# Input norm's factor multiplied onto the projection's results, the first two column groups taken together, and the filters' first layers in five overlapping steps

## The chip, the core and the metric

The kernel runs on one core of a Trainium2 chip, as one program on five engines: TensorE (PE) multiplies matrices, VectorE (DVE) and ScalarE (ACT) work elementwise, GpSimd (POOL) helps with a few elementwise steps, and SyncE (SP) issues most of the transfers. The metric is the device time of one execution in microseconds (us), the median of several runs. All engines run their own list of instructions in order and wait for each other through semaphores.

## The reference, cut to what matters

One encoder layer over 2048 positions of width 1024, all in float32. The part that the change touches is its beginning: a norm over the rows of the input, one wide projection, a width-3 convolution over the positions, and the network that makes the filters of the long convolutions.

```python
def _rms_norm(x, g):
    y = xf * lax.rsqrt(jnp.mean(xf * xf, axis=-1, keepdims=True) + EPS)
    return (y * g.astype(jnp.float32)).astype(x.dtype)
...
        u = _rms_norm(h, norm_mix_g[l])
        proj = u @ w_in[l]
        hy = _short_conv_centred(proj[..., :HY_COLS], hy_conv_w[l], hy_conv_b[l])
...
    hid = jnp.sin(fr1.astype(f32) * (z @ w1.astype(f32) + b1.astype(f32)))
    hid = jnp.sin(fr2.astype(f32) * (hid @ w2.astype(f32) + b2.astype(f32)))
    filt = (hid @ w3.astype(f32)).reshape(L, HYENA_ORDER, FILTER_DIRS, D_HYENA)
```

After that come the long convolutions (the hyena group) by transforms of 64 by 64 points, a gated recurrence over chunks (mLSTM), an output projection, cross-attention into 256 memory tokens and a squared-ReLU feed-forward layer. None of these is changed.

## The kernel before, in words

**Two-part products.** A float32 operand is split into a high part (`xh`, `wh`) in the matmul's own type and the rest (`xl`, `wl`). Each product is three matmuls (`mm3`, lines 340 to 342): high by high, high by low, low by high. For the split, ScalarE writes the high part and VectorE subtracts it from the source (`split`, line 345).

**The sweep.** `sweep` makes the projection transposed, with output channels on partitions and positions along the free axis. It goes by column groups `c2` of 256 channels. For each, four accumulations of 24 matmuls of 128x512 each are made: `c` is one of two chunks of 512 positions, `m` one of two halves of the 256 channels. I call one such accumulation a product group; it fills one of four `mm` banks of the matmul memory. A group's result is copied by ScalarE into a row buffer `P` (line 687). When both chunks of a channel block are there, the width-3 convolution is made from `P` into `cv` (one ScalarE and two VectorE instructions, lines 701 to 704), and later `sweep_out` transposes `cv` on TensorE and writes it out. The program makes the first half of the positions (`hf` = 0) for column groups 0 to 3, then the second half for the same ones: 16 and 16 product groups. Between the two, `x_chunk` loads and normalises the other 1024 positions into the same `xh` and `xl`.

**The beginning.** `x_first` loads 512 positions of x (`x0`), sums the squares over the 1024 channels (ScalarE squares, VectorE adds, one small matmul over the partitions, line 539), takes the inverse root on VectorE with eleven instructions of four columns (`rsqrt`), spreads the 512 factors over all partitions by a matmul with a diagonal (`spread`, line 456), multiplies x by gain and factor (`gained`, line 464), and only then splits it into `xh` and `xl`. The other 512 positions (`x1`) are treated the same; their sums come from a second copy of x in its natural layout, which ScalarE squares and sums along the rows (`square_sum`, line 421).

**The filters.** `filters` first makes the hidden layer `hid` in four column pieces, each with two matmuls (lines 267 and 271) and two sines; a sine is six VectorE instructions and one of ScalarE. Then come 32 steps: two matmuls into `pf` and `pb` (`hy<-fw,hid`), two VectorE multiplications by the decay window (lines 317 and 318), a sum on VectorE (line 322), a difference on GpSimd, and four transform matmuls (`hy<-b,f`).

**What sets the order.** `program` weaves generators by hand-set weights: the sweep with the filters, then the hyena group with the rest of the projections. A scheduler then reorders the instructions by its own simulated times within what data and buffers allow, except those pinned by `keep_in_program_order`. The hyena group begins with `spectrum` (line 879 on): 32 matmuls `hy<-a,f`, whose inputs are read from and whose results are written to device memory.

Of the kernel before, what the change touches and what calls it, by code (L numbers as in the profile page):

```python
# [10 lines left out]
F32 = mybir.dt.float32  # L11
# [122 lines left out]
class Prog:  # L134
    def __init__(self, ctx, tc, a):
# [19 lines left out]
        self.mid = None  # L155
# [78 lines left out]
    def filters(self):  # L234
# [3 lines left out]
        if True:  # L238
            fw = sb.tile([128, 1280], F32, name="fw")
            nc.scalar.dma_start(out=fw, in_=a["fw"])  # L240
# [3 lines left out]
            nc.scalar.dma_start(out=f1, in_=a["c_f1"])  # L244
# [16 lines left out]
            for c in range(4):  # L261
                yield 2
                cs = slice(512 * c, 512 * c + 512)
                feat = tb()
                nc.sync.dma_start(out=feat[0:66], in_=a["c_feat"][:, cs])
                p1 = self.hy()
                nc.tensor.matmul(p1, w1, feat[0:66], start=True, stop=True)
                hid1 = tb()
                sine(hid1, p1, 0, 1, c == 0)
                p2 = self.hy()  # L270
                nc.tensor.matmul(p2, w2, hid1, start=True, stop=True)
                sine(hid.rearrange("p j (g m) -> p m g j", g=2)[:, 16 * c:16 * c + 16], p2, 2, 3)
# [215 lines left out]
    def x_first(self):  # L488
        nc, sb = self.nc, self.isb
        pin = self.tc.keep_in_program_order  # L490
        c0, c1 = slice(0, 512), slice(512, 1024)

        def write(xs, cs, rb, between=lambda k: None):
            for k in range(9):
                if k < 8:
                    d = self.gained(xs[k], self.g_mix[:, k:k + 1], rb)
                    if k:
                        pin(d)
                    pin(nc.scalar.copy(self.xh[:, k, cs], xs[k]))
                if k:  # L500
                    nc.vector.tensor_tensor(self.xl[:, k - 1, cs], xs[k - 1], self.xh[:, k - 1, cs].bitcast(F32), ALU.subtract)
                between(k)

        def pieces(ts):
            return [ts[k // 2][:, k % 2] for k in range(8)]

        x0 = []
# [4 lines left out]
        wsrc = self.items[0][0].rearrange("(k p) c -> p k c", p=128)  # L512
        w0 = [sb.tile([128, 8, 256], F32R, tag=tag, name=tag, bufs=2) for tag in ("wh", "wl")]
        raw = [self.ta().rearrange("p k c -> p (k c)").rearrange("p (k c) -> p k c", k=4) for i in range(2)]
        for i in range(2):
            nc.sync.dma_start(out=raw[i], in_=wsrc[:, 4 * i:4 * i + 4])
        nat = []
        for i in range(4):
            rows = self.a["x"][512 + 128 * i:640 + 128 * i]
            if i < 2:  # L520
                xn = sb.tile([128, D], F32, tag="xn", name="xn", bufs=2)
                nc.sync.dma_start(out=xn, in_=rows)
                nat += [xn[:, 0:512], xn[:, 512:1024]]
            else:
                for h in range(2):
                    xn = self.tb()
                    nc.sync.dma_start(out=xn, in_=rows[:, 512 * h:512 * h + 512])
                    nat.append(xn)
        x1 = pieces([self.x_load(1, j, self.ta()) for j in range(4)])

        ssum = sb.tile([128, 512], F32, tag="rb", name="ssum", bufs=2)
        for k in range(8):
            sq = sb.tile([128, 512], F32, tag="st", name="sq", bufs=3) if k else ssum
            pin(nc.scalar.activation(sq, x0[k], AF.Square))
            if k:
                nc.vector.tensor_tensor(ssum, ssum, sq, ALU.add)
        p = self.mm()
        for t in range(4):
            nc.tensor.matmul(p[:, t:t + 1], ssum[:, 128 * t:128 * t + 128], self.ones[:, 0:1], start=True, stop=True)
        self.inv_rms(self.rx[:, 0:4], p[:, 0:4])  # L540
        dg = self.diagonal(self.rx[:, 0:4])
        ss = sb.tile([128, 2, 4], F32, tag="ss", name="ss", bufs=2)

        def nat_sum(i):
            self.square_sum(nat[i], ss[:, i % 2, i // 2:i // 2 + 1])

        for k in range(0, 8, 2):
            ks = slice(k, k + 2)
            self.split(w0[0][:, ks], w0[1][:, ks], raw[k // 4][:, k % 4:k % 4 + 2])
        for i in range(4):  # L550
            nat_sum(i)
        self.wst = iter((w0,))
        rb = self.spread(dg)
        later = []

        def between(k):
            if k < 4:
                nat_sum(4 + k)
            if k == 4:
                self.close_sums(self.rx[:, 4:8], ss)  # L560
                later.append(self.diagonal(self.rx[:, 4:8]))
        write(x0, c0, rb, between)

        def rest():
            write(x1, c1, self.spread(later[0], True))
            w1 = self.weights(sb, *self.items[1], kc=2, nbufs=4, pin=True)
            self.wst = self.stream(sb, self.items[2:], w1, kc=2, nbufs=4)
        self.mid = rest
        for _ in range(9):
            yield  # L570
        for c in (2, 3):
            yield from self.row_stats(self.rx[:, 4 * c:4 * c + 4], self.a["x"][512 * c:512 * c + 512])
        yield from self.row_stats(self.rm, self.a["mem"])

    def pop(self, n=1):
        for _ in range(n):
            if self.prepq is not None and next(self.prepq, 0) == 0:
                self.prepq = None

# [74 lines left out]
    def sweep(self, cols, hf, first, after=None):  # L654
        nc, a, sb = self.nc, self.a, self.isb
        xh, xl, cw, cb, carry = self.xh, self.xl, self.cw, self.cb, self.carry
        for c2 in cols:
            wh, wl = next(self.wst)
            Ps = []
# [6 lines left out]
            for c in range(2):  # L666
                for m in range(2):
# [5 lines left out]
                    for k in range(8):  # L673
                        self.mm3(p, wh[:, k, ms], wl[:, k, ms], xh[:, k, cs], xl[:, k, cs], k == 0, k == 7)
                        if k == 5 and self.mid is not None:
                            f, self.mid = self.mid, None
                            f()
                    if c == 0:
                        P = sb.tile([128, 1088], F32, tag="P", name="P", bufs=2)
                        Ps.append(P)  # L680
                        edge = 0 if hf == 0 else 1024 if first else 1041
                        nc.vector.memset(P[:, edge:edge + 1], 0.0)
                        if not first:
                            e0 = 1025 if hf == 0 else 0
                            nc.vector.tensor_copy(P[:, e0:e0 + 17], cc)
                    P = Ps[m]
                    nc.scalar.copy(P[:, off + 512 * c:off + 512 * c + 512], p)
                    if c == 0:
                        if self.pending:
# [1323 lines left out]
```

## Time and profile before

| | us |
|---|---|
| median of 3 runs | 3173.7 |
| lowest and highest run | 3167.94 and 3176.09 |
| profiled execution | 3171.69 |
| its span from first to last instruction | 3169.9 |

TensorE counts as busy in 3035.0 us of the span (96%), VectorE in 2048.8, ScalarE in 1499.1. In the views below, a timeline row gives start and duration, the engine, the line of the code, the operation, output and inputs by the program's tile names, and in brackets how long the engine had stood idle and for whom. A row of a table of stages gives the length of the stage, the busy time of TensorE, of its weight loads, of VectorE, ScalarE and GpSimd with their counts, TensorE's granted clock, the share of the transfer engines that was in use, and GB/s.

### The profile page before, as it was taken

What the parts mean: (1) busy time and instruction counts of PE and PEld (TensorE: products, weight loads), DVE (VectorE), ACT (ScalarE), POOL (GpSimd) and SP (SyncE); (2) the same over time, 40 slices, a digit from 0 to 9 for tenths busy, and PEclk for the clock granted to TensorE, in tenths of its full rate; (3) what the DMA queues carried; (4) which work ended last, traced back from release to release, by engine and by line L of the source; (5) the groups of instructions that cost most, each with busy time, mean ns of one, the idle gap of its engine ahead of it and who ended that gap; (6) DMA issues with size and microseconds to landing.
All of it is one profiled execution on the core that took longest, in us unless ns stands there. A gap on an engine that the chain in (4) does not pass through costs nothing.

```text
span 3169.9 us, 43590 instructions
## 1 busy us (share of the span) xinstructions
PE 3035.0 (96%) x14473; PEld 2391.2 (75%) x14473; DVE 2048.8 (65%) x3563; ACT 1499.1 (47%) x2873; POOL 1155.0 (36%) x802
## 2 busy tenths in 40 slices
PE   6999999999899986999999999999999999999998
PEld 4655666876577866888888888888888778888876
DVE  7775466344755787877765656557555685565595
ACT  5533366424555444554454455556555443333335
POOL 0122012100112234323141426776555483434483
PEclk9999999999999988999999999999999999999999
DMA  5564877685677988546384747656644474444434
GB/s 188 191 208 160 266 204 209 176 262 183 176 217 209 275 271 258 170 147 230 122 273 147 262 138 247 206 193 225 213 146 150 167 243 145 146 127 150 124 92 170
DMA packets 447530, 609.22 MB, mean 192 GB/s; under 512 B 39102, under 2 KB 249150, under 8 KB 446280
## 3 DMA queue, kind: packets, MB, share of 16 engines
q1 hardware_dynamic: 409124, 547.92, 54.3%
q10 hardware_dynamic: 38180, 58.51, 5.6%
q8 instruction: 115, 1.88, 0.2%
q14 instruction: 111, 0.91, 0.1%
HBM read 403.88 MB, written 202.41 MB: 191 GB/s over the span
## 4 chain that ended last, share of the span: by engine, by line
PE 78%; DVE 7%; DMA 7%; ACT 3%; issue 3%; POOL 2%; SPq 0%; ACTq 0%; DVEq 0%; POOLq 0%
PE mm L340 17%; PE mm L342 17%; PE mm L341 16%; PE hy L340 5%; PE hy L342 5%; PE hy L341 5%; PE hy L177 3%; PE mm L842 1%; DVE wl L345 1%; PE hy L873 1%; PE hy L915 1%; DMA xt<-in_x_t_dram 1%; PE hy L1079 1%; DVE bl L1547 1%; PE hy L1202 1%
## 5 line engine op out<-in xcount | busy, mean ns | idle before, releaser
L345 DVE TENSOR_TENSOR wl<-wn,wh 128x512 fp32r<-128x512 f32 (+1 forms) x364 | 289.8, 839 | 99.7 <-ACT wh L345 97.8
L1547 DVE TENSOR_TENSOR bl<-wr,bh 128x512 fp32r<-128x512 f32 x213 | 239.5, 1130 | 128.8 <-ACT bh L1546 127.7
L1546 ACT CAST ah<-w 128x512 fp32r<-128x512 f32 x284 | 176.6, 623 | 302.9 <-PE hy L341 155.2
L920 POOL TENSOR_TENSOR b<-b,a 128x512 f32<-128x512 f32 x64 | 87.0, 1362 | 578.5 <-ACT b L918 484.0
L340 PE MATMUL mm<-xh,wh 128*128 128x512 f32 x640 | 274.2, 429 | 7.2 <-DVE st L205 2.8
L345 ACT CAST wh<-wn 128x512 fp32r<-128x512 f32 (+1 forms) x364 | 205.2, 618 | 154.0 <-PE mm L342 52.4
L342 PE MATMUL mm<-xh,wl 128*128 128x512 f32 x640 | 257.8, 404 | 0.0
L341 PE MATMUL mm<-xl,wh 128*128 128x512 f32 x640 | 255.7, 400 | 0.0
L1546 ACT CAST bh<-wr 128x512 fp32r<-128x512 f32 x232 | 143.7, 621 | 231.2 <-PE mm L342 175.1
L1547 DVE TENSOR_TENSOR al<-w,ah 128x512 fp32r<-128x512 f32 x236 | 215.2, 912 | 54.5 <-ACT ah L1546 54.5
L342 PE MATMUL mm<-bh,al 128*128 128x512 f32 x576 | 225.3, 394 | 7.6 <-DVE al L1547 4.8
L340 PE MATMUL mm<-bh,ah 128*128 128x512 f32 x576 | 226.9, 394 | 1.8 <-DVE acc L1704 1.7
L341 PE MATMUL mm<-bl,ah 128*128 128x512 f32 x576 | 226.1, 392 | 0.0
L341 PE MATMUL mm<-act,wh 128*128 128x512 f32 x512 | 200.4, 392 | 0.2 <-DVE act L345 0.2
L342 PE MATMUL mm<-act,wl 128*128 128x512 f32 x512 | 198.9, 391 | 0.0
L340 PE MATMUL mm<-act,wh 128*128 128x512 f32 x512 | 198.4, 394 | 0.2
L340 PE MATMUL hy<-bh,ah 128*128 128x512 f32 x448 | 175.2, 391 | 0.0
L341 PE MATMUL hy<-bl,ah 128*128 128x512 f32 x448 | 174.6, 390 | 0.0
L342 PE MATMUL hy<-bh,al 128*128 128x512 f32 x448 | 174.4, 390 | 0.0
L340 PEld LDWEIGHTS mm<-xh,wh 128*128 128x128 f32 x640 | 122.4, 191 | 65.6 <-issue 19.8
L340 PE MATMUL mm<-wh,xh 128*128 128x256 f32 (+1 forms) x512 | 154.1, 302 | 6.9 <-ACT xh L345 5.1
L341 PEld LDWEIGHTS mm<-xl,wh 128*128 128x128 f32 x640 | 121.8, 190 | 48.1 <-issue 23.7
(377 smaller groups left out, 8381.0 us busy)
## 6 DMA issues: line engine op xcount, KB each, us to landing
wr<-hc SPq DMA_DIRECT2D x224, 256.0 KB
w<-in_ff_w_dram SPq DMA_DIRECT2D x172, 256.0 KB
hc<-wn SPq DMA_DIRECT2D x128, 256.0 KB
wn<-in_w_in_dram SPq DMA_DIRECT2D x100, 256.0 KB
hc<-q SPq DMA_DIRECT2D x96, 256.0 KB
fs<-a SPq DMA_DIRECT2D x32, 512.0 KB
a<-fs SPq DMA_DIRECT2D x64, 256.0 KB
a<-zs SPq DMA_DIRECT2D x64, 256.0 KB
```

The lines of the kernel that those rows point to most:

```text
L177: b = self.nc.tensor.matmul(*products[-1], start=True, stop=True)
L340: mm(ps, lh, rh, start=start, stop=False)
L341: mm(ps, lh, rl, start=False, stop=False)
L342: mm(ps, ll, rh, start=False, stop=stop)
L345: both = (self.nc.scalar.copy(hi, src), self.nc.vector.tensor_tensor(lo, src, hi.bitcast(F32), ALU.subtract))
L842: nc.tensor.matmul(pp, dm[:, m], t[:, m], start=True, stop=True)
L873: nc.tensor.matmul(pg, em[:, m], y, start=True, stop=True)
L915: nc.tensor.matmul(pp, dm[:, m], t[:, m], start=True, stop=True)
L920: nc.gpsimd.tensor_tensor(xt, xt, hi[:, m], ALU.mult)
L1079: pin(nc.tensor.matmul(pc[:, 129 * i:129 * i + 129], kk[:, 2 * p + i], ve[:, 2 * p + i], start=True, stop=True))
L1546: self.nc.scalar.copy(hi, src)
L1547: eng.tensor_tensor(lo, src, hi.bitcast(F32), ALU.subtract)
```

## The change

**The factor moves.** In `x_first` the operand is now x times the gain alone: ScalarE writes `xh` with the gain as its scale, VectorE writes `xl` in one instruction that multiplies and subtracts. The row factor is multiplied onto the results instead: VectorE multiplies each of the first 16 product groups by `rowb` while it moves them out of the matmul memory, where ScalarE copied them before. Squares and sums of both chunks are now made from the transposed x (the natural copy is no longer loaded), after the operands.

**Two column groups together.** For the first 1024 positions, column groups 0 and 1 run together: the four product groups of chunk 0 first, then the four of chunk 1. Up to three finished groups wait in their banks before they leave (`lag`). `hooks` puts the loads, squares and factors between the matmuls of these groups, by group and step. The weights of group 1 are loaded with those of group 0.

**The filters' hidden layer** runs in five steps, in each of which one piece's first layer and the piece before's second layer are made. Its weights and the transform matrix are now loaded by SyncE, behind x, and the sweep is five groups ahead before it starts, where it was two.

```diff
-            nc.scalar.dma_start(out=fw, in_=a["fw"])
+            nc.sync.dma_start(out=fw, in_=a["fw"])
...
+            for c in range(5):
+                yield 6
+                last = hid1
+                if c < 4:
+                    p1 = self.hy()
+                    nc.tensor.matmul(p1, w1, feats.pop(0)[0:66], start=True, stop=True)
+                if c:
+                    p2 = self.hy()
+                    nc.tensor.matmul(p2, w2, last, start=True, stop=True)
+                if c < 4:
+                    hid1 = tb()
+                    sine(hid1, p1, 0, 1, c == 0)
+                if c:
+                    sine(hid.rearrange("p j (g m) -> p m g j", g=2)[:, 16 * c - 16:16 * c], p2, 2, 3)
...
+            x0.append(self.x_load(0, j, t[:, 0:D].rearrange("p (k t) -> p k t", k=2)))
+            if j % 2 == 0:
+                nc.sync.dma_start(out=raw[j // 2], in_=wsrc[:, 2 * j:2 * j + 4])
...
+        def operand(xs, c, k):
+            to = (slice(None), k, slice(512 * c, 512 * c + 512))
+            g = self.g_mix[:, k:k + 1]
+            pin(nc.scalar.activation(self.xh[to], xs[k], AF.Copy, scale=g))
+            nc.vector.scalar_tensor_tensor(self.xl[to], xs[k], g, self.xh[to].bitcast(F32), ALU.mult, ALU.subtract)
...
+        def columns(c):
+            p = self.hy()
+            for t in range(4):
+                nc.tensor.matmul(p[:, t:t + 1], ssum[c][:, 128 * t:128 * t + 128], self.ones[:, 0:1], start=True, stop=True)
+            rx = self.rx[:, 4 * c:4 * c + 4]
+            self.inv_rms(rx, p[:, 0:4])
+            self.dg = self.diagonal(rx)
+
+        def rows(c):
+            p = self.hy()
+            nc.tensor.matmul(p, self.ones, self.dg, start=True, stop=True)
+            nc.scalar.copy(self.rowb[c], p)
...
+        self.hooks = {(0, 5): second, (1, 5): operands, (2, 0): lambda: scales(0), (2, 5): lambda: squares(x1, 1),
+                      (4, 0): lambda: scales(1), (6, 0): third}
...
+        for run in [cols[:2]] + [[c2] for c2 in cols[2:]] if self.made == 0 else [[c2] for c2 in cols]:
...
+            for c, c2 in [(c, c2) for c in range(2) for c2 in run]:
...
-                    nc.scalar.copy(P[:, off + 512 * c:off + 512 * c + 512], p)
...
+                        if hf == 0 and first:
+                            nc.vector.tensor_tensor(to, p, self.rowb[c], ALU.mult)
+                        else:
+                            nc.scalar.copy(to, p)
...
+                    self.lag.append(leave)
+                    while len(self.lag) > max(0, min(3, 8 - self.made)):
+                        self.lag.pop(0)()
+                    self.made += 1
...
-            next(s)
-            next(s)
-            weave(s, p.filters(), 140, 80, True)
+            f = p.filters()
+            for _ in range(5):
+                next(s)
+            next(f)
+            weave(s, f, 140, 102, True)
```

How the instructions stand now, at three places. First SyncE's queue at the start of the program, where `xt` are the four pairs of x's first chunk, `a<-in_w_in` the halves of the first weights, `xn` and `b` the natural copy of x, `a<-in_x_t` the second chunk, `wn` the next weights. Before:

```order
L475 DMA xt<-in_x_t_dram 128x2x512 x4
L516 DMA a<-in_w_in_dram 128x4x256 x2
L522 DMA xn<-in_x_dram 128x1024 x2
L527 DMA b<-in_x_dram 128x512 x4
L475 DMA a<-in_x_t_dram 128x2x512 x4
L374 DMA wn<-in_w_in_dram 128x2x256 x4
```

And now:

```order
L486 DMA xt<-in_x_t_dram 128x2x512
L519 DMA a<-in_w_in_dram 128x4x256
L486 DMA xt<-in_x_t_dram 128x2x512 x2
L519 DMA a<-in_w_in_dram 128x4x256
L486 DMA xt<-in_x_t_dram 128x2x512
L560 DMA wn<-in_w_in_dram 128x2x256 x4
L486 DMA a<-in_x_t_dram 128x2x512 x4
L240 DMA fw<-in_fw_dram 128x1280
L244 DMA f_358<-in_c_f_dram 128x128
```

The first weights moved to second place in the queue, the natural copy is gone, and the filters' weights stand behind the second chunk.

Second, VectorE's list around the first row factors. Before, the diagonal of the first chunk (`dg`) is followed by the operand products `xt<-xt,par,rb` and the residuals `xl`:

```order
L417 COPY small<-xr_y 128x4
L450 TENSOR_SCALAR dg<-ident,small 128x128 x4
L464 SCALAR_TENSOR_TENSOR xt<-xt,par,rb 128x512 x2
L501 TENSOR_TENSOR xl<-xt,xh 128x512
L464 SCALAR_TENSOR_TENSOR xt<-xt,par,rb 128x512
```

Now the diagonal comes behind all 16 residuals, and four results (`P`, `P_97`, `P_98`) are multiplied by the row factors `rowb_95` right after it, ahead of the second chunk's sum of squares (`ssum_94`) and the next weights:

```order
L428 COPY small<-xr_y 128x4
L461 TENSOR_SCALAR dg<-ident,small 128x128 x4
L706 TENSOR_TENSOR P<-mm,rowb_95 128x512 x2
L706 TENSOR_TENSOR P_97<-mm,rowb_95 128x512
L706 TENSOR_TENSOR P_98<-mm,rowb_95 128x512
L533 TENSOR_TENSOR ssum_94<-ssum_94,sq 128x512 x7
L356 TENSOR_TENSOR wl<-wn,wh 128x512 x2
```

The release of the four banks moved from ScalarE's list to VectorE's, behind the factor's chain.

Third, TensorE's list where the hyena group's first transforms (`hy<-a,f`, 32 in all) stand among the sweep's matmuls (`mm<-xh,wh` and its like) and transposes (`mm<-ident,cv`). Before, at the 912th sweep matmul:

```order
L342 MATMUL mm<-xh,wl 128x512
L721 MATMUL mm<-ident,cv 126x128 x3
L177 MATMUL hy<-a,f_2447 128x512
L188 MATMUL hy<-a,f_2447 128x512
L721 MATMUL mm<-ident,cv 126x128 x3
L177 MATMUL hy<-a,f_2447 128x512
L188 MATMUL hy<-a,f_2447 128x512
L721 MATMUL mm<-ident,cv 126x128 x2
```

Now, at the 960th, where 28 of the 32 stand in one piece (its end is shown):

```order
L177 MATMUL hy<-a,f_2481 128x512
L188 MATMUL hy<-a,f_2481 128x512
L866 MATMUL mm<-a,dm 128x512 x2
L351 MATMUL mm<-xh,wh 128x512
L352 MATMUL mm<-xl,wh 128x512
L353 MATMUL mm<-xh,wl 128x512
```

Before, the 32 began behind the 868th sweep matmul and ended behind the 950th; now they begin behind the 949th and end behind the 960th.

More of the change, by code (lines that the diff above doesn't have):

```diff
@@ L517, in x_first @@
[L517 to L528, printed above, removed]
@@ L540, in x_first @@
[L540 to L553, printed above, removed]
@@ L554, in x_first @@
[L554 to L567, printed above, removed]
```

168 lines of the change are left out of this document (89 added, 79 removed).

## Prediction

> **What bounds the kernel now.** The page comes first. TensorE is busy almost everywhere, so only the places where it is not can be gained or lost.
>
> ```profile
> span 3169.9 us, 43590 instructions
> PE 3035.0 (96%) x14473; PEld 2391.2 (75%) x14473; DVE 2048.8 (65%) x3563; ACT 1499.1 (47%) x2873; POOL 1155.0 (36%) x802
> ```
>
> Next the table of stages over the part that the change touches, with one later stage and two stretches chosen for VectorE.
>
> ```profile
> 0.00:20.00 20.00, 2.01 (x9) 1.92 (x9) 11.32 (x35) 10.76 (x21) 0.70 (x6) 1.00 0.92 336
> 20.00:40.00 20.00, 13.95 (x25) 7.03 (x26) 15.97 (x41) 9.45 (x19) 0.00 (x0) 0.85 0.54 191
> 60.00:80.00 20.00, 18.69 (x86) 14.49 (x86) 15.89 (x28) 14.60 (x31) 0.00 (x0) 1.00 0.66 185
> 80.00:100.00 20.00, 19.01 (x85) 14.98 (x84) 16.63 (x40) 14.50 (x32) 0.00 (x0) 1.00 0.79 265
> 140.00:160.00 20.00, 15.75 (x78) 8.54 (x76) 20.00 (x47) 12.45 (x18) 3.11 (x2) 1.00 0.57 190
> 160.00:180.00 20.00, 18.71 (x67) 9.47 (x68) 19.15 (x33) 6.09 (x10) 4.82 (x3) 0.83 0.59 202
> 200.00:220.00 20.00, 20.00 (x104) 11.72 (x106) 13.29 (x20) 8.22 (x16) 5.71 (x4) 1.00 0.56 185
> 347.00:390.00 43.00, 41.00 (x169) 22.96 (x169) 19.11 (x30) 15.86 (x28) 0.00 (x0) 1.00 1.01 334
> 0.00:164.65 164.65, 132.77 (x554) 93.21 (x555) 125.44 (x265) 86.63 (x162) 11.97 (x12) 0.97 0.58 192
> 143.30:164.65 21.35, 15.81 (x68) 8.41 (x67) 21.35 (x40) 10.56 (x16) 4.28 (x2) 0.89 0.58 192
> ```
>
> TensorE does almost nothing in the first 20 us. Around 140 to 180, where x's second half is prepared, VectorE is full (20.00 and 19.15 of 20) and TensorE is not. After 200 TensorE is full again. The waits (for whom: total, times, longest) name the same two places:
>
> ```profile
> PE hy L271 <- ACT b L258: 3.9, 1, 3.9
> PE mm L456 <- DVE dg L450: 3.9, 1, 3.9
> PE hy L177 <- DVE b L318: 3.6, 1, 3.6
> ```
>
> The timeline gives the beginning:
>
> ```profile
> 5.48 0.63 ACT L534 ACTIVATE ssum<-xt 128x512 f32<-128x512 f32 x1 [1.95 <-DMA xt<-in_x_t_dram]
> ...
> 8.71 1.15 ACT L534 ACTIVATE sq<-xt 128x512 f32<-128x512 f32 x2 [2.08 <-DMA xt<-in_x_t_dram]
> ...
> 10.03 1.15 ACT L534 ACTIVATE sq<-xt 128x512 f32<-128x512 f32 x2 [0.17 <-DMA xt<-in_x_t_dram]
> ...
> 14.10 1.87 PE L539 MATMUL mm<-ones,ssum 128*128 128x1 f32 x8 [14.10 <-DVE ssum L536]
> ...
> 16.00 0.16 DVE L416 TENSOR_SCALAR ms<-mm 128x4 f32<-128x4 f32 x1 [0.15 <-PE mm L539]
> ...
> 18.93 0.87 DVE L450 TENSOR_SCALAR dg<-ident,small 128x128 f32<-128x128 f32 x4
> 19.86 2.08 PE L456 MATMUL mm<-dg,ones 128*128 128x512 f32 x2 [3.89 <-DVE dg L450]
> 21.97 0.59 ACT L460 COPY rb<-mm 128x512 f32<-128x512 f32 x1 [3.84 <-PE mm L456]
> ...
> 24.05 0.80 PE L340 MATMUL mm<-xh,wh 128*128 128x512 f32 x1 [2.11 <-ACT xh L499]
> ...
> 27.50 0.63 PE L341 MATMUL mm<-xl,wh 128*128 128x512 f32 x1
> ...
> 42.40 0.39 PE L340 MATMUL mm<-xh,wh 128*128 128x512 f32 x1
> 42.63 0.39 PE L341 MATMUL mm<-xl,wh 128*128 128x512 f32 x1
> ```
>
> The first sweep product starts at 24.05, behind squares, sums, root, diagonal and spreading. The ninth starts at 27.50, so the first ones are 0.43 apart; at 42.40 they are 0.23 apart.
>
> **The change, part by part.** I first follow the new beginning to the first multiplication of the second chunk's results, then VectorE's work from there to the reload of x, then TensorE.
>
> *Beginning.* The first pair of x lands by 5.5 and further transfers of the same size 1.3 apart (8.71 to 10.03), so the first weights, now second in the queue, land near 6.8 and TensorE starts near 7. Root and spreading no longer stand before it. The filters' weights, moved behind x, are needed only by the filters, which start behind 190 products; that cover costs nothing. The first two groups (48 products) need 12 at 0.43 and 36 at 0.23, 13.4 us, so they end at 20.4; the sixth transfer lands at 12, so they do not wait for it. In TensorE's new list the column sums stand behind product 76 (26.8). I take 1 us for them, half of 1.87, since that row ran at the slow spacing. The root and diagonal take 3.8 (16.00 to 18.93 and 0.87), to 31.5. The spread stands behind product 94, at 31.9, and takes 1 (half of 2.08); ScalarE's copy 0.6. The first row factor is there at 33.5, and the fifth group waits about 1 us for the first bank, to 34.2. Products 97 to 142, the second column sums, products 143 to 186 and the second spread follow: 10.4 + 1 + 10 + 0.9, to 56.6; with the copy, the multiplication of the fifth group starts at **57.5**. VectorE has long finished the second diagonal by then and waits: its list stands behind that spread.
>
> *VectorE's work.* Its prices, by group (busy in total, mean ns of one):
>
> ```profile
> L464 DVE SCALAR_TENSOR_TENSOR xt<-xt,par,rb 128x512 f32<-128x512 f32 x24 | 17.4, 764 | 4.1 <-ACT rb L460 2.8 <-DMA xt<-in_x_t_dram 1.3
> L345 DVE TENSOR_TENSOR wl<-wn,wh 128x512 fp32r<-128x512 f32 x20 | 12.9, 689 | 1.0 <-ACT wh L345 1.0
> L703 DVE SCALAR_TENSOR_TENSOR cv<-P,par,cv 128x1008 f32<-128x1008 f32 x8 | 10.1, 1266 | 4.8 <-ACT cv L701 4.8
> ...
> L322 DVE TENSOR_TENSOR b<-b 128x512 f32<-128x512 f32 x11 | 8.6, 786 | 0.4
> L317 DVE TENSOR_TENSOR b<-hy,a 128x512 f32<-128x512 f32 x11 | 7.6, 688 | 9.0 <-PE hy L188 9.0
> ...
> L501 DVE TENSOR_TENSOR xl<-xt,xh 128x512 fp32r<-128x512 f32 x8 | 5.4, 688 | 0.7 <-ACT xh L499 0.7
> L536 DVE TENSOR_TENSOR ssum<-ssum,sq 128x512 f32<-128x512 f32 x7 | 4.8, 692 | 7.0 <-ACT sq L534 6.5
> ```
>
> The fused residual and the multiplication of a result are not in this trace. The first is bounded by 0.69 (a plain residual) and 0.76 (the two-step `xt` product); I take 0.76, the same form. The second is bounded by 0.69 (`b<-hy,a`, a product with one input in the matmul memory) on both sides within a few hundredths, for shape and types are the same. Up to the fourth wide split of the reload, which ends at 164.65, VectorE had 125.44 us of work. Its new list has, up to the same split: 16 gain products less (12.2), 16 plain residuals less (11.0), three filter steps less, which moved behind (6 at 0.69 and 3 at 0.79, 6.5); 16 fused residuals (12.2), 16 results (11.0), 7 sums (4.8), 8 diagonals (1.7) and one `cv` (1.3) more. That is 31.0 - 29.7, so 126.7 us. Ahead of 57.5 stand 16 fused residuals, 12 `wl`, 14 sums, 8 diagonals, 4 results and 26 small ones of 0.16: 12.2 + 8.3 + 9.7 + 1.7 + 2.8 + 4.2 = 38.9. So 87.8 us are left, and the split ends at 57.5 + 87.8 = **145.3** if VectorE never waits. It was full from 143.30 to 164.65; I take 2 us of waits, between none and 20 (its share in 60 to 100 was 81%; a rival below). ScalarE is no limit: it loses 16 copies and eight row sums and was at 14.6 of 20 at most.
>
> *TensorE.* The second half's first 18 products follow that split; here is where it stood:
>
> ```profile
> 171.48 0.79 PE L340 MATMUL mm<-xh,wh 128*128 128x512 f32 x1
> ```
> ```profile
> L340 PE MATMUL mm<-xh,wh 128*128 128x512 f32 x136 | 57.5, 426 | 4.0 <-ACT xh L499 2.1 <-ACT xh L345 1.9
> ```
> ```profile
> L188 PE MATMUL hy<-fw,hid 64*128 64x512 f32 x64 | 36.6, 655 | 0.0
> ...
> L188 PE MATMUL hy<-b,f 64*64 64x512 f32 x192 | 36.1, 616 | 0.0
> ```
>
> 136 of each of the three products lie before 171.48, so this is the 409th. Now six products follow the split: 145.3 + 2 + 1.4 = 148.7, which is 22.8 earlier. But by then TensorE had done 16 `hy<-fw,hid` and 24 `hy<-b,f`, and has now done 6 and 6. All 64 of the first kind take 36.6 us (two engine rows each) and all 128 of the second 36.1, so 10 x 0.57 + 18 x 0.28 = 10.8 us are still owed. The lead is 12.0 us, and since TensorE is full from 200 on, it stays until the hyena group begins.
>
> *The hyena group's first stage.* Before, 32 `hy<-a,f` lay among 82 sweep products, and the transfer engines were at 1.01 for 43 us at 334 GB/s:
>
> ```profile
> 347.61 0.69 PE L177 MATMUL hy<-a,f 64*128 64x512 f32 x1
> ```
> ```profile
> L188 PE MATMUL hy<-a,f 64*128 64x512 f32 x32 | 16.9, 628 | 0.0
> ```
>
> Now they lie among 11 products, so about 16 us of cover are gone. The stage reads 8 x 0.5 MB and writes 16 x 0.5 MB; four reads can come ahead and three pairs of writes may end behind it, which leaves 7 MB, 21 us at 334 GB/s, against 16.9 + 2.5 us of matmuls. So the loss is between none and 16 (the stage keeps its 43 us); I take 1.4, close to the 21.
>
> Sum: 22.8 - 10.8 - 1.4 = 10.6 us against the profiled execution of 3171.7 (2 us under the median of 3173.7): **3161.1 us**. 0.3% is 9.5 us here, about what a measurement of this kernel can tell from no change.
>
> **A rule against it.** The granted clock was 0.85 in 20 to 40 and the first products were 0.43 apart for over 3.4 us. If the operands of the first two groups come with gaps and the clock stays down for all 48 products, they take 20.6 instead of 13.4, and all that follows, VectorE's wait for the second spread too, comes 7.2 later: gain 3.4, 3168. The first products before had such gaps and stayed slow for six microseconds. Against it: the new operands come every 0.7 us for two groups at once, more than slow products can use. The Trainium skill ("TensorE: Matmul & The Clock Gate", Part 1) says that the clock is halved until a whole busy window of about 3.4 us, running free of the kernel, has passed. By that page the slow stretch here would be an estimated 3.4 to 6.8 us, 8 to 16 products, which moves the sum by 1 us to either side.
>
> **Rivals.**
>
> *The lead is eaten on the way.* VectorE waits more than I take, or the hyena's first stage loses half of its cover. For: TensorE now waits for banks that VectorE's list frees in order, and 28 transforms stand in one piece. Against: full VectorE at 143 to 164, and reads that can run ahead. With 8 us of the 16 lost in that stage, 3161.1 + 6.6 = 3168; with VectorE at 92%, 6 us more, 3167.
>
> *Slower: VectorE and TensorE wait for each other in turn.* Twelve groups, the fifth to the sixteenth, now leave their banks only through VectorE's list, where sines and convolutions stand ahead of them; TensorE stops for a bank, and VectorE then stops for what TensorE has not yet made. Place: 57 to 165. If VectorE is busy only 78% of that, its 87.8 us take 112.6, 24.8 of waits instead of 2: 3161.1 + 22.8 = **3184**. It decides from 22 us of waits on, a share below 80%. For: 15.89 and 16.63 of 20 in 60 to 100, under an order made by the same rules. Against: there TensorE was the fuller one (18.69, 19.01), so VectorE could not be; when it was behind, it was full.
>
> *The clock stays down*: 3168, as above.
>
> **How the numbers follow.** The forecast has 0.47, the eaten lead 0.28, the slow clock 0.08, the mutual waits 0.17. So faster by over 0.3% 0.47, within 0.3% 0.36, slower 0.17. The forecast's own range is 3156 to 3164: no waits and no loss gives 3157.7, with 2 us for the early walk; 3 us more of waits the upper end. The range over all cases is **3154 to 3180**: below lies only an early walk that is wrong by more than 3 us (0.06), above most of the mutual waits (0.12).
>
> **What would show it.** TensorE's first sweep product near 7 us; the first multiplication onto a result near 33.5 and the fifth near 57.5; VectorE at 95% or more from there to the fourth wide split, near 147; the 409th product near 149, with 6 and 6 filter products before it; the 28 transforms in 18 to 23 us. The forecast is wrong if VectorE has idle times over 10 us in all between 57 and 147, if the transforms take 30 us or more, or if TensorE's total idle time from 400 us on, in the stages that are worded the same, grows by more than 5 us.

## The result, and the profile after

The changed kernel takes 3149.7 us (median of 6 runs, 3146.7 to 3152.8), the kernel before 3172.5 (also 6 runs): ratio 0.993, interval 0.9918 to 0.9943. So it is faster by 22.7 us, where the forecast had 10.6 (3161.1 against the profiled execution's 3171.7), and lies below the range. The two profiled executions, on which all that follows rests, took 3171.7 and 3152.8 us. First the page, whose span was 3169.9 before:

```profile
span 3151.0 us, 43589 instructions
PE 3025.6 (96%) x14481; PEld 2387.9 (76%) x14481; DVE 2054.8 (65%) x3569; ACT 1490.3 (47%) x2848; POOL 1149.4 (36%) x802
```

TensorE's work is the same, so the question is where it loses time. I count its work by giving every matmul the median distance to the next one of its kind and shape in the two kernels (2904 us in all); what a stretch takes beyond that is lost, to waits and to a slow clock alike. From here on "lost" means this. Each figure comes from one execution. Up to 340 us, kernels with the same TensorE list differ by at most 1.7 us in it. Behind the last place where lists differ (1307 to 1359 us) all fourteen kernels of this study have the same one and need 1829 to 1833 us for it. But 17 runs of the kernel before lie between 3160.0 and 3177.7 us, so a few us in one stage between 340 and 1360 prove little.

| us lost in | 0 to 200 | 200 to 340 | 340 to 420 | 420 to 700 | 700 to 1000 | 1000 to 1300 | 1300 to 3100 |
|---|---|---|---|---|---|---|---|
| before | 59.7 | 31.9 | 8.8 | 10.6 | 37.8 | 76.2 | 24.0 |
| after | 49.6 | 32.6 | 24.2 | 9.0 | 14.6 | 74.1 | 26.0 |
| difference | -10.1 | +0.7 | **+15.4** | -1.6 | **-23.2** | -2.1 | +2.0 |

The 10.1 us of the beginning, for which the forecast had 12.0, are used up by 420. The gain is made between 700 and 1000, in instructions that the change leaves as they were. The differences add up to -18.9 us, as the two spans do. The table of stages shows the same, first before, then after (behind the stage and its length comes TensorE's busy time; the last three numbers are its granted clock, the share of the transfer engines and GB/s):

```profile
340.00:420.00 80.00, 76.18 (x316) 49.37 (x315) 40.03 (x61) 35.87 (x59) 3.81 (x3) 1.00 0.89 273
700.00:1000.00 300.00, 279.70 (x1300) 200.63 (x1301) 172.44 (x365) 149.09 (x255) 41.35 (x33) 0.97 0.67 194
```
```profile
340.00:420.00 80.00, 64.58 (x271) 40.88 (x271) 33.67 (x52) 28.36 (x49) 4.29 (x3) 0.96 0.87 281
700.00:1000.00 300.00, 294.30 (x1396) 211.10 (x1396) 187.59 (x394) 161.16 (x274) 47.20 (x36) 0.99 0.76 219
```

*The beginning.* TensorE's timeline after, and VectorE's first multiplications of results:

```profile
8.97 0.80 PE L351 MATMUL mm<-xh,wh 128*128 128x512 f32 x1 [8.97 <-ACT wh L356]
...
13.83 0.63 PE L353 MATMUL mm<-xh,wl 128*128 128x512 f32 x1
14.25 0.67 PE L351 MATMUL mm<-xh,wh 128*128 128x512 f32 x2
14.76 0.39 PE L352 MATMUL mm<-xl,wh 128*128 128x512 f32 x1
...
84.52 2.07 PE L276 MATMUL hy<-b,fw 128*128 128x512 f32 x2 [6.35 <-ACT b L258]
```
```profile
36.00 2.49 DVE L706 TENSOR_TENSOR P<-mm,rowb 128x512 f32<-128x512 f32 x4 [2.39 <-ACT rowb L546]
60.37 1.89 DVE L706 TENSOR_TENSOR P<-mm,rowb 128x512 f32<-128x512 f32 x3 [6.58 <-ACT rowb L546]
```

The first product starts at 8.97, not near 7, since ScalarE loads a table (1.28 us) and makes a high part of x and of the weights first. The multiplications come at 36.0 and 60.4 (forecast 33.5 and 57.5). The slow stretch lasts from 8.97 to 14.25, 5.3 us with matmuls 0.43 apart, and none follows among the first 48 products: the rival of 48 slow products is out. The Trainium skill ("TensorE: Matmul & The Clock Gate", Part 1) has a busy window of about 3.4 us as the condition, in a window that runs free of the kernel; the 5.3 us lie within the 3.4 to 6.8 us estimated from it.

The lead is already largest at 60 us, 18 us, and falls to 8 by 100:

```profile
60.00:80.00 20.00, 17.36 (x76) 12.56 (x74) 19.63 (x38) 15.06 (x31) 0.00 (x0) 1.00 0.54 169
80.00:100.00 20.00, 13.89 (x45) 9.24 (x46) 16.58 (x55) 10.81 (x27) 0.00 (x0) 0.74 0.87 256
```
```profile
60.37:153.26 92.89, 80.29 (x333) 55.62 (x332) 85.33 (x188) 47.86 (x86) 4.21 (x2) 0.91 0.58 179
```

VectorE is full up to 80 (19.63 of 20), TensorE waits 6.35 us for a sine (row 84.52) and 1.6 for a step of a root (`ms`), and its granted clock falls to 0.74. This is close to the rival of mutual waits, but over 40 us, not 100, and for the filters' sines: for a bank that a multiplication of results frees, TensorE waits 0.4 us in all from 60 to 153. To the fourth wide split, which ends at 153.3 instead of 147.3, VectorE does 85.3 us of work in 92.9 (92%), where I had 87.8 and 2 us of waits. The 409th product starts at 145.4 (forecast 149, with the 6 and 6 filter products that were named), 7.9 us before that split ends; so it does not hang on the split, as the forecast's working has it, and TensorE's list takes other products first.

*The transforms.* They last from 360.8 to 392.5. Over that time, and TensorE's waits from 340 to 420:

```profile
360.80:392.50 31.70, 19.73 (x74) 8.20 (x75) 15.59 (x24) 11.66 (x21) 0.00 (x0) 0.95 1.04 349
```
```profile
PE hy L177 <- DMA a<-hy: 6.1, 3, 3.8
PE hy L177 <- ACT a L909: 5.8, 4, 1.9
```

With the transfer engines at 1.04 and 349 GB/s, TensorE has work for 19.7 of 31.7 us. In that time 11.1 MB were moved (31.7 times 349), not the 7 MB of the forecast.

What opens this stage is not TensorE. Its first reads (`a<-hy`) stand in SyncE's queue behind a wait for the landing of the filters' last result (`fs<-a`); as the code has it, the hyena group's pool of buffers is opened where the filters' one was closed. The reads before, then SyncE's wait and the reads after:

```profile
340.66 2.54 SPq L818 DMA_DIRECT2D a<-hy  x4
```
```profile
SPq L835 <- DMA fs<-a: 3.4, 1, 3.4
353.97 2.44 SPq L842 DMA_DIRECT2D a<-hy  x4
```

The filters start three groups later in the changed kernel, and this landing comes at 352.9 instead of 339.6. In all fourteen kernels the first read is issued 0.9 to 1.1 us behind it. Meanwhile TensorE goes on with sweep products: 838 had started when the first read was issued before, 920 now. That work is then missing beside the transforms as cover, that is, as work for TensorE while the transfers run.

*From 700 to 1000.* The longest waits before, and all above 0.3 us after:

```profile
PE mm L340 <- ACT xh L345: 5.1, 3, 3.2
PE mm L721 <- DVE a L846: 3.3, 1, 3.3
PE mm L340 <- DVE st L205: 2.8, 2, 2.3
PE mm L842 <- DMA a<-fs: 2.4, 1, 2.4
PE mm L842 <- DVE a L846: 1.9, 1, 1.9
```
```profile
PE mm L351 <- ACT xh L356: 3.5, 2, 2.7
PE mm L351 <- ACT st L203: 1.8, 1, 1.8
PE hy L897 <- DMA va<-vd: 1.5, 1, 1.5
```

The first row, waits for an operand, mostly stays. What goes are the waits for `mm` banks that VectorE empties (`a`, results of the hyena group's filter responses; `st`, transposed pieces). Such a wait can cost more than itself, as before at 798 and at 843:

```profile
797.72 0.69 PE L721 MATMUL mm<-ident,cv 128*128 128x128 f32 x4 [3.31 <-DVE a L846]
799.79 0.37 PE L727 MATMUL mm<-ident,cv 128*16 128x128 f32 x1 [1.38 <-DVE a L846]
...
803.89 0.63 PE L341 MATMUL mm<-xl,wh 128*128 128x512 f32 x1
804.32 0.63 PE L342 MATMUL mm<-xh,wl 128*128 128x512 f32 x1
...
843.27 0.80 PE L340 MATMUL mm<-xh,wh 128*128 128x512 f32 x1 [2.35 <-DVE st L205]
843.87 0.63 PE L341 MATMUL mm<-xl,wh 128*128 128x512 f32 x1
844.29 0.63 PE L342 MATMUL mm<-xh,wl 128*128 128x512 f32 x1
```

Matmuls are 0.43 apart behind the first wait until 805, and behind the one at 843 until 846; the granted clock was 0.50 from 800 to 805 and from 843 to 846. The stretch from 780 to 820 loses 9.2 us for 5.6 us of waits. The Trainium skill ("TensorE: Matmul & The Clock Gate", "Why this matters for your kernels") warns of gaps over about 3 us; the wait of 3.31 us agrees, but here 2.35 us, behind a few short transposes, were enough.

### The profile page after: what moved, and what is told of

It is laid out like the page before. It is cut to its first block, busy times and chain, and to the rows that moved or that the text cites. A ratio compares the mean times of both kernels' runs of the same rounds, so it can differ in the third digit from the quotient of the medians.

```text
span 3151.0 us, 43589 instructions
## 1 busy us (share of the span) xinstructions
PE 3025.6 (96%) x14481; PEld 2387.9 (76%) x14481; DVE 2054.8 (65%) x3569; ACT 1490.3 (47%) x2848; POOL 1149.4 (36%) x802
## 4 chain that ended last, share of the span: by engine, by line
PE 79%; DVE 8%; DMA 6%; ACT 3%; issue 2%; SPq 1%; POOL 0%; ACTq 0%; DVEq 0%; POOLq 0%
PE mm L353 17%; PE mm L351 17%; PE mm L352 17%; PE hy L353 5%; PE hy L351 5%; PE hy L352 5%; PE hy L177 3%; PE hy L897 1%; PE mm L866 1%; PE hy L939 1%; DVE wl L356 1%; DVE bl L1571 1%; DMA xt<-in_x_t_dram 1%; PE hy L1226 1%; DVE xt L475 1%
## 5 line engine op out<-in xcount | busy, mean ns | idle before, releaser
L351 PE MATMUL mm<-xh,wh 128*128 128x512 f32 x640 | 267.2, 419 | 13.3 <-ACT wh L356 9.0
L334 POOL TENSOR_TENSOR b<-b 128x512 f32<-128x512 f32 x32 | 54.1, 1692 | 289.4 <-DVE b L331 145.9
```

What stands on the lines that cost most here:

```text
L334: nc.gpsimd.tensor_tensor(e[1], f, b, ALU.subtract)
L351: mm(ps, lh, rh, start=start, stop=False)
```

## Experiments

Two theories for the late gain. A: it comes from how far the sweep has been handed out when the hyena group begins. The weaving takes 28 of its 32 groups before and 29 now, and the scheduler makes another order of what stands behind. B: it comes from the new beginning. Each kernel was timed beside the kernel before on the same chip (medians 3171.6 us for experiments 1 to 4, 3170.7 for 5 to 8, 3170.1 for 9 to 12).

**1. One number back.**

```diff
-            weave(s, f, 140, 102, True)
+            weave(s, f, 133, 102, True)
```

> The changed kernel with one number turned back: the sweep is handed out in the ratio 133 to 102 against the filters instead of 140 to 102, so that as many of its product groups (28) as in the kernel before stand ahead of the hyena group, where it is 29 now. Beginning, filters and factors stay as changed. Theory A (the time won between 700 and 900 us comes from how far the sweep has been handed out when the hyena group begins, not from the new beginning): TensorE's idle time between 700 and 1000 us rises from 14.6 us to about 37.8, as in the kernel before, and the kernel takes about 3173 us; the first 32 transforms now stand in one piece, so the loss there stays at 15 us or grows by 2. Theory B (it comes from the new beginning and what its results wait for): the idle time there stays near 15 us and the time near 3150 us.

3179.4 us, ratio 1.0024 (1.0015 to 1.0033): the gain is gone and more. TensorE's list is that of the changed kernel to 358 us and nothing differs up to 340 (lost 81.4, after 82.2); from 700 to 1000 it loses 34.9. Its waits there are those of the kernel before again:

```profile
PE mm L351 <- ACT xh L356: 3.5, 3, 2.0
PE mm L745 <- DVE a L870: 3.4, 1, 3.4
PE mm L351 <- DVE st L205: 2.8, 2, 2.4
PE mm L866 <- DMA a<-fs: 2.2, 1, 2.2
PE mm L866 <- DVE a L870: 1.9, 1, 1.9
```

Theory B falls. The whole gain of the change hangs on this number.

**2. The new beginning alone** (factor on results, two groups together), with filters and weaving of the kernel before:

```diff
...
-            f = p.filters()
-            for _ in range(5):
-                next(s)
-            next(f)
-            weave(s, f, 140, 102, True)
+            next(s)
+            next(s)
+            weave(s, p.filters(), 140, 80, True)
```

> The new beginning alone: the factor on the results and two column groups together as in the changed kernel, but the filters' hidden layer, its loads and the weaving as in the kernel before. The first 32 transforms of the hyena group stand among 160 sweep matmuls. Theory A: the early lead of about 10 us stays and is not lost in the transforms, but nothing is won between 700 and 900 us: 3172 - 10 = 3162 us, within 4. Theory B: the 23 us between 700 and 900 are there as well: about 3140 us.

3188.6 us, ratio 1.005 (1.0035 to 1.0065). Both expectations miss: it is slower, by 17 us. It loses 72.8 us to 200, 13.1 more than before. The longest waits of TensorE to 200 (the second is the one before its first product):

```profile
PE hy L534 <- DVE dg L450: 10.0, 2, 5.2
PE mm L340 <- ACT wh L345: 10.0, 1, 10.0
PE hy L271 <- ACT b L258: 8.0, 3, 4.4
```

In one list, the new beginning's factors (`dg`) and the filters' sines (`b`) hold TensorE in turn: something like the rival of mutual waits, though for no bank, and VectorE is busy for 14.6 and 12.0 us of 20 from 60 to 100. From 700 to 1000 it loses 38.2, with 28 groups.

**3. The filters' part alone** on the beginning of the kernel before: `filters` and the five lines of `program` as changed, nothing else.

> The other part alone: the kernel before with its own beginning, but the filters' hidden layer in five steps, their loads on SyncE and the new weaving (five groups ahead, 140 to 102). The transforms stand among 96 sweep matmuls. Theory A: no early lead (within 4 us), no loss beyond that of the kernel before in the transforms, and the 23 us between 700 and 900 are won: about 3150 us. Theory B: about 3172 us.

**3138.1 us**, ratio 0.9893 (0.9876 to 0.991): faster than the changed kernel by 11.6 us (10.8 if each is set against the kernel before on its own chip). Theory A's time misses by 12. It loses 50.5 us to 200, as little as the changed kernel (49.6), 18.6 from 340 to 420, and 11.1 from 700 to 1000. So an early lead of 9.2 us, where theory A expects none, is had without TensorE's early start, to which I gave it. The transforms lose 9.8 more than in the kernel before, where none was expected.

**4. The changed kernel with earlier filters.**

```diff
-            for _ in range(5):
+            for _ in range(2):
                 next(s)
             next(f)
-            weave(s, f, 140, 102, True)
+            weave(s, f, 154, 102, True)
```

> The changed kernel, with the filters started two product groups into the sweep instead of five and a ratio of 154 to 102, so that 29 groups stand ahead of the hyena group as now. The 28 transforms that stand in one piece in the changed kernel are spread over 108 sweep matmuls. If the 15 us lost between 340 and 420 us come from the missing cover of those transforms' transfers, this loss falls to that of the kernel before (5 us or less), and the time to about 3137 us, less or more by what the earlier filters do to the beginning (4 us). If the transfers bound that stage whatever stands between them, the loss stays and the time is near 3150 us.

3139.9 us, ratio 0.9899 (0.9885 to 0.9914). From 340 to 420 it loses 8.2 instead of 24.2, as expected from the cover; 7.9 more are lost to 200.

**5. One number in the kernel before.**

```diff
-            weave(s, p.filters(), 140, 80, True)
+            weave(s, p.filters(), 146, 80, True)
```

> The kernel before with one number changed: the sweep is handed out against the filters in the ratio 146 to 80 instead of 140 to 80, so that 29 product groups instead of 28 stand ahead of the hyena group. Nothing of the change itself is in it. Theory A (the gain of the late stages comes from this position alone): nothing happens before 340 us, TensorE's idle and slow time between 700 and 1000 us falls from 37.8 us to about 12, and the time is 3172 - 24 = 3148 us, within 6. Rival (the late gain needs the five filter steps or the new beginning as well): the time stays within 5 us of 3172.

3165.2 us, ratio 0.998 (0.9968 to 0.9993). Nothing differs to 340, and from 700 to 1000 it loses 17.4, 20.4 less, with no part of the change: A holds for that stage. But 12.3 are lost again from 1000 to 1300 (88.5), and 2.9 in the transforms, so the total moved by 5.5, not 24, and the time is neither theory's.

**6 and 7. The filters alone, two groups ahead, with 29 and 30 groups** (`range(2)`; 154 and 160 to 102).

> The filters' part alone on the old beginning, as in the run of the filters alone, but started two groups into the sweep instead of five and handed out 154 to 102, which again puts 29 groups ahead of the hyena group. The hyena group's first transforms begin 46 sweep matmuls earlier. If the 18.6 us that the filters alone lose between 340 and 420 us come from transforms that stand late (14 of 32 behind the 948th sweep matmul), the loss falls to that of the kernel before (9 us) and the time from 3138 to about 3129 us; if the old beginning is disturbed by filters that start earlier, as the new one was (7 us), it stays at 3136 to 3145 us.

> The run before it with the ratio 160 to 102, which puts 30 groups ahead of the hyena group instead of 29; the order up to the transforms is the same. If every group that the sweep is ahead wins time between 700 and 1000 us, another 5 to 20 us are won there; if 28 to 29 was a single step (one particular collision that goes away), the time is within 5 us of that of 29 groups.

3141.9 (ratio 0.9912, 0.9893 to 0.9932) and 3159.9 us (0.997, 0.9956 to 0.9984). With 29 groups the transforms lose 12.1 instead of 18.6, but 6.7 more go to 200: no net gain. With 30, 23.2 are lost from 700 to 1000 (13.1 with 29), and the time is 18 us above that of 29 groups, which neither expectation had: between 28 and 30 there is one good place, not a slope. From 1000 to 1300 it loses 89.0, with 29 groups 74.0.

**8. Without the multiplications.** ScalarE copies the first 16 results; the factor is left out of them.

```diff
-                        if hf == 0 and first:
-                            nc.vector.tensor_tensor(to, p, self.rowb[c], ALU.mult)
-                        else:
-                            nc.scalar.copy(to, p)
+                        nc.scalar.copy(to, p)
```

> The changed kernel without the 16 multiplications of results by the row factor: ScalarE copies the first 16 product groups out of their banks, as in the kernel before (the factor itself is still made, and not used). The results are not normalised in this run, only its time counts. Theory V (the lead of the new beginning, 18 us at 60 us, is used up between 70 and 100 us because VectorE's list, with these multiplications and the filters' sines in it, holds TensorE): the 12.4 us lost there shrink to under 5 and the lead at 200 us grows from 10 to 17 us or more. Rival S (the filters' hidden layer itself, a chain of matmul, six VectorE steps and a sine per piece, sets that wait): the loss stays at 10 us or more, wherever the hidden layer now stands, and the lead at 200 us stays within 3 us of 10.

The lead at 200 is 21.5 us, as theory V has it; from 70 to 100, 6.5 are still lost, not under 5. Yet the run takes 3158.6 us (0.9959, 0.9945 to 0.9973), since 43.2 are lost from 340 to 420. The sweep has run out there: TensorE stands still for 8.4 us before the first transform (at 360.7), whose reads were issued at 354.7, when the filters' last result had landed (353.7). The scheduler also placed the filters later, so experiment 10 has that alone.

**9. Two loads on the other queue.** The kernel of experiment 3 with

```diff
-            nc.sync.dma_start(out=fw, in_=a["fw"])
+            nc.scalar.dma_start(out=fw, in_=a["fw"])
...
-            nc.sync.dma_start(out=f1, in_=a["c_f1"])
+            nc.scalar.dma_start(out=f1, in_=a["c_f1"])
```

> The filters' part alone, with their two loads issued by ScalarE at the start as in the kernel before; the order of TensorE's list is nearly the same. The filters alone were 3.7 us ahead of the kernel before already at 40 us. If that comes from the moved loads (0.7 MB that no longer stand ahead of x), it is gone here, and the time is 3 to 5 us above the 3138 us of the filters alone; if the five steps make it, the time stays within 2 us of 3138.

3155.2 us (0.995, 0.9933 to 0.9966), 17 us above experiment 3, which neither expectation had. But the loads cost only 2.3 us at 40, of which 0.5 is left at 1000. The rest is lost behind 1000. The table of stages for experiment 3, then for this one:

```profile
0.00:1000.00 1000.00, 959.77 (x4564) 665.86 (x4565) 609.67 (x1119) 503.82 (x870) 149.32 (x107) 0.99 0.69 209
1000.00:1200.00 200.00, 176.13 (x1123) 147.84 (x1122) 155.41 (x336) 95.76 (x200) 79.44 (x55) 0.95 0.89 277
1200.00:1300.00 100.00, 84.52 (x459) 74.16 (x458) 85.73 (x231) 47.12 (x148) 41.95 (x31) 0.88 0.67 214
```
```profile
0.00:1000.00 1000.00, 958.33 (x4562) 664.99 (x4563) 609.76 (x1119) 503.91 (x870) 148.65 (x107) 0.99 0.69 209
1000.00:1200.00 200.00, 172.34 (x1113) 144.03 (x1112) 153.63 (x312) 93.24 (x186) 75.05 (x52) 0.94 0.89 274
1200.00:1300.00 100.00, 69.45 (x366) 60.80 (x365) 75.45 (x218) 38.84 (x129) 33.42 (x26) 0.80 0.59 189
```

In TensorE's list the two differ in the first part of the sweep, and then again only where the recurrence begins among the memory's products. In experiment 3 (left) the third piece of the recurrence (`qn,kk_t`, four for a piece) follows at once on the first two; here (right) the memory's products (`wh,kt`) come ahead of it:

```
L1175 MATMUL hy<-qn,kk_t 128x128 x8          L1175 MATMUL hy<-qn,kk_t 128x128 x4
L1213 MATMUL hy<-va,rw 128x129 x5            L1213 MATMUL hy<-va,rw 128x129 x5
...                                          ...
L1090 MATMUL hy<-ve,kn 128x129 x4            L351 MATMUL mm<-wh,kt 128x512 x4
L1175 MATMUL hy<-qn,kk_t 128x128 x4          L352 MATMUL mm<-wl,kt 128x512
```

TensorE's waits from 1200 to 1310 there, first experiment 3, then this one:

```profile
PE hy L1213 <- DVE ht L1248: 5.2, 2, 4.1
PE hy L1350 <- DVE act L356: 2.8, 1, 2.8
```
```profile
PE hy L1213 <- DVE bry L215: 9.1, 2, 4.6
PE hy L1090 <- issue: 7.4, 1, 7.4
PE hy L1213 <- DVE ht L1248: 5.8, 2, 3.4
```

**10. Late filters with the multiplications** (`range(8)`, 122 to 102 in the changed kernel).

> The changed kernel with the filters started eight groups into the sweep instead of five, ratio 122 to 102, again 29 groups ahead of the hyena group. The filters' steps now stand where they stand in the run without the factor (transforms from the 460th sweep matmul on), but the 16 multiplications of results stay on VectorE. Theory V (those multiplications hold TensorE): 12 us or more are lost between 60 and 200 us beyond the run without the factor, and the lead over the kernel before at 200 us stays near 10 us. Rival S (the place of the filters decides): the lead at 200 us comes out near 21 us, as without the factor. Either way the transforms stand in one piece behind the 960th sweep matmul, so more than 24 us are lost between 340 and 420 us, and the time is over 3150 us.

3189.8 us (1.0062, 1.0045 to 1.0078). The lead at 200 is 15.3 us, between both theories: with filters at the same place the multiplications cost 21.5 - 15.3 = 6.2 us, and the place of the filters gives 15.3 - 10.1 = 5.2, each to within 2 us or so. The lead is lost again: 41.8 us from 340 to 420, 10.9 of them waiting for the reads before the first transform.

**11 and 12. 480 instead of 499** in the weaving of the hyena group with the rest, in the kernels of experiments 5 and 3.

```diff
-                      279, 499)
+                      279, 480)
```

> The kernel before with two numbers changed: 146 to 80 as in the run of that number alone, and 279 to 480 instead of 279 to 499 for the hyena group against the rest of the projections. This brings the first pieces of the recurrence between the memory's products at the same place as in the changed kernel (behind 432 of their 480 matmuls, where the run of 146 to 80 alone has 425, 432 and 456). If this place makes the difference between 1000 and 1300 us (88.5 us lost in the run of 146 to 80, 70 to 74 in the kernels with that place), the loss there falls to 70 to 78 and the time from 3165 to about 3152 us; if not, it stays above 84 there.

> The filters' part alone with 279 to 480 for the hyena group against the rest. The first pieces of the recurrence now stand behind 369 of the memory's 480 products instead of 432, and 14 of the first transforms behind the 936th sweep matmul. If the recurrence between 1000 and 1300 us gains from more cover, 5 to 15 us are won there against the 70 us of the filters alone, and the time falls to 3125 to 3133 us; if the one step from 28 to 29 groups was needed in the stage from 700 to 1000 us and 480 takes it back, 20 us are lost there and the time is near 3155 us.

3166.5 (0.9989, 0.9977 to 1.0001) and 3148.6 us (0.9934, 0.9917 to 0.995). The first still loses 84.3 from 1000 to 1300 though the first pieces of the recurrence stand where they stand in the changed kernel, so that place alone is not the cause. The second loses 76.0 there, not less than 70.0, and 21.3 from 700 to 1000: the best kernel of the study stays that of experiment 3.

Three stages, over all fourteen kernels (before, after and the twelve experiments):

- 340 to 420, by the number of sweep matmuls ahead of the first transform: 776: 3.6 lost; 842: 7.4 and 12.1; 862: 8.2; 868: 8.8 (before), 11.7, 11.9; 888: 16.9, 17.1, 18.6; 936: 27.2; 949: 24.2 (after); 960: 41.8, 43.2, the two in which the sweep has run out.
- 700 to 1000, by groups handed out: 28: 34.9, 37.8 (before), 38.2; 29: 11.1 to 23.5, ten kernels (after 14.6; the two with 480: 20.0 and 21.3); 30: 23.2.
- 1000 to 1300: 70.0 to 78.2 in eight kernels, before and after among them; 83.4 to 89.7 in six.

## Why the prediction was wrong

It had the direction, but its number came from the wrong place. Step by step:

- *Start, factors, second chunk*: 8.97, 36.0 and 60.4 against 7, 33.5 and 57.5. All 2 to 3 us late, right in kind.
- *VectorE to the fourth wide split*: the work was right (85.3 us against 87.8), the waits 7.6 instead of 2, and the split ended at 153.3.
- *The lead of 12.0 us*: 10.1 were measured at 200. That it comes from TensorE's early start was wrong. The filters' part alone gives 9.2, and the new beginning alone loses 13.1. Together the beginning adds 0.9: most of its 18 us at 60 go where the filters' sines and the multiplications (6.2 us, experiments 8 and 10) share VectorE's list. The old beginning with filters eight groups late was not run, so what the new beginning is worth by itself there stays open.
- *The hyena group's first stage, 1.4 us*: mis-sized; 15.4 were measured, the upper end of my 0 to 16. I took it from transfers of 7 MB in 21 us; 11.1 MB were moved in 31.7, with little beside them. The list over the fourteen kernels shows that the loss grows, though not strictly, with the sweep products done ahead of the first transform, and experiment 4 that it falls to 8.2 when the transforms are spread among sweep products again. My working let the stage begin earlier by TensorE's lead; it begins when the filters' last result has landed, which is later now. So the lead was work done early, not time won; experiment 8 has the most lead (21.5) and the most loss (43.2). The test I named, 30 us or more for the transforms, came true for all 32 (31.7); the 28 in one piece alone took 27.0, not 18 to 23.
- *Everything behind 420 us at nothing*: this is the step that put the time outside the range. I took the stages as unchanged since their instructions are; but the scheduler orders them anew up to about 1300 us, and one group more ahead of the hyena group removes most of the loss of 700 to 1000 (experiments 1 and 5, one number each). -23.2 us stood against a term of zero, and no rival had it. That the other two errors, a lead 2 us too large and a stage 14 too cheap, worked against it brought the time nearer to the forecast by luck.
- *The rivals*: the eaten lead happened, completely. Something like the mutual waits happened for 40 us, and helps to make experiment 2 slower. The slow clock over the first 48 products did not happen.

Open: what sets the loss from 1000 to 1300. Experiments 3 and 9 show that two loads at the start change the order at the beginning of the recurrence, and 19.7 us with it; experiment 11 shows that the place of its first pieces does not explain it alone. In four of the six kernels with the larger loss (experiments 5, 7, 9 and 10) the third piece stands 24 of the memory's products behind the first two, and in none of the eight with the smaller one; but experiment 11 loses as much with the three together.

## What to carry to other kernels

Work that is done early is a gain only if nothing later uses it as cover: ask what opens the next stage that is bound by transfers (here the end of another stream, on another queue), what stands beside it, and how much of that the lead removes. Where a scheduler orders the program, a change at the start can move stages a thousand microseconds later by 20 us either way; so test its parts alone, and put the hand-set numbers of the old kernel to the same trial (one number gave 5.5 us here, and the filters' part alone beat the whole change by 11.6). Don't credit a part with a gain that stands in another stage.

## What the runs showed of the hardware that was not expected

Short waits of TensorE cost more than their length. Two of 3.3 and 1.4 us close together, with two of under 0.5 behind them, lost 9.2 us in that stretch (780 to 820), with matmuls 0.43 apart instead of 0.23 until 805. One of 2.35 us was followed by 2.7 us at half the clock (843 to 846). That two loads on another queue go with 17 us is not shown to be the chip's doing: 0.5 us of it stood at 1000, and the rest came where the scheduler had made another order.
